# Four column tiles for experts of up to 32 rows, and three split blocks ahead instead of two

## The chip, the cores and the metric

The kernel runs on one core of one Trainium2 chip. The metric is the device time of one execution in microseconds (us), taken as the median of several runs.

## What is computed

The reference is two transformer blocks, one after the other, on 512 tokens of 1024 channels. The first block is differential attention and a gated linear recurrence, merged, with an MLP behind. The second one is two kinds of attention, then a mixture of experts, then a gate. The change touches the mixture of experts alone, which is cut to this:

```python
# 512 tokens, D_MODEL = D_FF_2 = 1024, N_EXPERTS = 32, TOP_K = 4, SWIGLU_LIMIT = 7.0
logits = (xf @ w_router + b_router).astype(jnp.float32)
top_v, top_i = lax.top_k(logits, TOP_K)
w = jax.nn.softmax(top_v, axis=-1)
...
h = lax.ragged_dot(xs, w_up, sizes) + b_up[sorted_e]
g, lin = jnp.split(h, 2, axis=-1)
g = jnp.minimum(g, SWIGLU_LIMIT)
lin = jnp.clip(lin, -SWIGLU_LIMIT, SWIGLU_LIMIT)
act = g * jax.nn.sigmoid(SWIGLU_ALPHA * g) * (lin + 1.0)
y = lax.ragged_dot(act, w_down, sizes) + b_down[sorted_e]
y = y * w.reshape(-1)[order][:, None].astype(y.dtype)
return jax.ops.segment_sum(y, tok, num_segments=n).reshape(B, T, D)
```

The 2048 rows (512 tokens, four experts each) fall on the 32 experts as the data has it. With the inputs that are timed, 12 experts have over 64 rows (127 for the first in line, then 149, 143, 130, 126, 121, 101, 101, 87, 87, 82 and 74), and 20 have 64 or fewer: 9, 12, 19, 26, 29, 29, 29, 30, 31, 33, 36, and nine from 40 to 63.

## The kernel before

An expert's weights are 12 blocks of 1 MiB, eight of the upward product and four of the downward one (`ORDER`). Each block is fetched by one transfer on SP's queue (`fetch`, L1122) into one of eight raw buffers, block n into buffer n mod 8. So block n + 8 can be fetched when block n is done with; `refill(n)` does that. The raw buffers are halves of the tiles b1, pp, b3 and b0.

The experts stand in an order that the kernel computes on the chip from the row counts (`order`). Two forms of expert exist:

- A **large expert** (`expert`, over 64 rows) works on 128 rows in three products of split numbers. `unfold` splits a raw block into a high part (ACT, L219) and a low part (DVE, L220); four pairs of buffers hold such parts: two named wh and wl, one named raw, one in b2. `part` (L1316 the bias, L1322) then does 12 matmuls of 128x512 for a block: high by high, low by high, and high by the rows' low part. In the loop over its 12 blocks, the split of block i + 2 stands ahead of the matmuls of block i. In the first four pairs a large expert may have more than 128 rows; `second` does these with 16 matmuls of 128x128 a block, on four column tiles of 32 rows (L1476, L1482), directly from the raw block, which is refilled only then.
- A **small expert** (`few`, 64 rows or fewer) reads the raw blocks directly: `halves` (L1517 the bias, L1521) does eight matmuls of 128x256 a block on two column tiles of 64 rows each.

After the upward blocks 1, 3, 5 and 7 (small: 3, 5 and 7) follows the gate (`swiglu` or `gated`): steps on ACT (L1345, L1346) and on DVE (L1347 to L1349), then transposes on PE and a copy or split (`flip`) give the rows of the downward product. The last of these, after block 7, feeds blocks 10 and 11.

`places` runs the first expert, then a chain of nested conditions `pairs(t)` (L1235). In it a small expert and a large one alternate, the smallest with the largest first, while `nP > t`; nP, a count that the chip computes, is 11 for these inputs. I call them pair 1 to pair 11 (t = 0 to 10). The remaining small experts come out of a tree of conditions, `rest` (L1243). In a paired small expert, blocks 10 and 11 are followed by the splits of the next large expert's first two blocks, and its rows are flipped (`ahead`, L1303) at blocks 8 and 9. Instructions run in program order on each engine; a scheduler sets that order from the code when the program is built, within one arm of a condition.

Of the kernel before, what the change touches and what calls it, by code (L numbers as in the profile page):

```python
# [157 lines left out]
class K:  # L158
# [944 lines left out]
    RAW, PAIRS = 8, 4  # L1103
# [38 lines left out]
    def moe(self):  # L1142
        tc, nc, a = self.tc, self.nc, self.a
        with ExitStack() as es:
# [52 lines left out]
            for n in range(2):  # L1197
                self.unfold(n)
# [10 lines left out]
    def places(self, srt):  # L1209
# [41 lines left out]
        pairs(0)  # L1251
# [106 lines left out]
    def finish(self, e, big):  # L1358

        nc, m = self.nc, self.m  # L1360
        sl, i = m["sl"][e // 4 % 2], e % 4
        if big:
            for c in range(2):
                nc.scalar.activation(m["y"][0][:, 512 * c:512 * c + 512], self.bank(e, 8 + c), AF.Copy, scale=sl["w"][:, i:i + 1])
            self.scatter(m["y"][0], sl, i)
        else:
            for c in range(2):
                p, w = self.bank(e, 8 + c), sl["w"][:64, i:i + 1]
                nc.scalar.activation(m["y"][0][:64, 512 * c:512 * c + 256], p[:64, :256], AF.Copy, scale=w)
                nc.vector.tensor_scalar(m["y"][0][:64, 512 * c + 256:512 * c + 512], p[64:, :256], w, None, op0=OP.mult)  # L1370
            self.scatter(m["y"][0], sl, i, 64)
# [44 lines left out]
    def expert(self, e, two=False):  # L1416
# [7 lines left out]
        for i in range(12):  # L1424
            n = e * 12 + i
            if i < 10:
                self.split(*self.pairs[(n + 2) % self.PAIRS], self.raw(n + 2))
                if not two:
                    self.refill(n + 2)
            if i < 2 and not two:  # L1430
                self.refill(n)
# [5 lines left out]
            if i == 0 and e:  # L1437
                self.finish(e - 1, False)
# [6 lines left out]
        self.finish(e, True)  # L1445
# [59 lines left out]
    def halves(self, p, x, i, e):  # L1505
# [5 lines left out]
        o = p[:64, :256], p[64:, :256]  # L1511

        cut = lambda w, n: self.cut(w, up, j, n, 2)
# [425 lines left out]
```

## Time and profile before

| what | us |
|---|---|
| median of three runs (2597.35 to 2602.37) | 2599.8 |
| the profiled execution | 2600.15 |
| its span, first to last instruction | 2598.1 |
| first small expert starts | 1385.37 |
| last pair ends | 2214.8 |

The mixture of experts fills the stretch from about 1340 to 2490 us. A timeline row gives the start of an operation, its duration, its engine and line, the tiles that it writes and reads, how often it stands there in a row, and in brackets the idle time of the engine before it with what ended it. A matmul in 32-bit floats counts as two in such a row: "x32" on L1482 is one block's 16 matmuls. "PE" is the matrix engine, "mm", "lg" and "pv" are its accumulators, "SPq" is SP's queue of issued transfers. The start of the next small expert is the end of a pair.

### The profile page before, as it was taken

How to read it: one execution, taken by the hardware profiler on the slowest of the kernel's cores; microseconds unless marked ns; L12 is line 12 of the kernel's file. 1: busy time of each engine (PE TensorE's matmuls, PEld its weight loads, DVE VectorE, ACT ScalarE, POOL GpSimd, SP SyncE). 2: the span in 40 equal slices, each digit the busy share in tenths (PEclk: the TensorE clock that was granted, in tenths of full speed). 3: DMA queues.
4: the chain of work that ended last, by engine and by line, in shares of the span. 5: the costliest groups of instructions: out<-in, count | busy, mean ns of one | idle time of the engine just before them, and what ended most of it. 6: DMA issues, size and time to landing. Idle time of an engine off the chain costs nothing. (4 is left out here: it accounts for less than half of the span.)

```text
span 2598.1 us, 41846 instructions
## 1 busy us (share of the span) xinstructions
PE 2425.4 (93%) x17042; PEld 1941.2 (75%) x17042; DVE 1326.2 (51%) x2473; ACT 1043.5 (40%) x1578; POOL 174.5 (7%) x184
## 2 busy tenths in 40 slices
PE   7999999999999999999989999999999999788888
PEld 5789987898898898898976676666666666554557
DVE  6767753344333344557585466445656666121135
ACT  5755552223223324557353344334444444111133
POOL 0021100000000000000010010110001000000000
PEclk9999999999999999999979999999999999899999
DMA  4122222322222222220378889989999999799990
GB/s 160 65 90 78 74 70 89 127 86 88 98 93 86 98 70 83 75 71 17 109 271 324 305 317 333 341 301 367 381 378 392 385 403 373 294 399 400 407 376 33
DMA packets 86474, 552.63 MB, mean 213 GB/s; under 512 B 11799, under 2 KB 12951, under 8 KB 24936
## 3 DMA queue, kind: packets, MB, share of 16 engines
q1 hardware_dynamic: 71280, 508.33, 50.6%
q0 software_dynamic: 8352, 29.76, 4.7%
q10 hardware_dynamic: 6616, 11.53, 1.3%
q8 instruction: 142, 2.33, 0.4%
q14 instruction: 84, 0.69, 0.1%
HBM read 530.03 MB, written 19.55 MB: 212 GB/s over the span
## 5 line engine op out<-in xcount | busy, mean ns | idle before, releaser
L245 PE MATMUL mm<-b,wh 128*128 128x512 f32 (+1 forms) x1840 | 512.8, 365 | 1.7 <-ACT b L222 0.8
L245 PEld LDWEIGHTS mm<-b,wh 128*128 128x128 f32 x1840 | 328.8, 190 | 65.4 <-issue 3.4
L245 PE MATMUL mm<-b,wl 128*128 128x512 f32 (+2 forms) x920 | 335.2, 365 | 1.3 <-DVE wl L205 1.3
L245 PE MATMUL mm<-wh,b 128*128 128x256 f32 x1488 | 284.3, 287 | 1.5 <-DVE b L675 0.8
L205 DVE TENSOR_TENSOR wl<-raw,wh 128x2048 fp32r<-128x2048 f32 x81 | 185.5, 2290 | 176.2 <-ACT wh L204 176.2
L204 ACT ACTIVATE wh<-raw 128x2048 fp32r<-128x2048 f32 x81 | 155.1, 1915 | 261.2 <-PE mm L245 248.8
L245 PEld LDWEIGHTS mm<-wh,b 128*128 128x128 f32 x1488 | 235.9, 191 | 4.6 <-DVE b L675 1.2
L245 PE MATMUL mm<-wl,b 128*128 128x256 f32 x744 | 213.0, 286 | 1.0 <-DVE wl L205 1.0
L220 DVE TENSOR_TENSOR wl<-b,wh 128x2048 fp32r<-128x2048 f32 x74 | 169.2, 2288 | 65.4 <-ACT wh L219 62.4
L245 PEld LDWEIGHTS mm<-b,wl 128*128 128x128 f32 (+1 forms) x920 | 174.6, 190 | 31.8 <-DVE wl L205 2.2
L1521 PE MATMUL lg<-b,xf 128*64 128x256 f32 x1280 | 154.3, 389 | 14.7 <-DMA b<-w_up 10.1
L219 ACT ACTIVATE wh<-b 128x2048 fp32r<-128x2048 f32 x74 | 141.0, 1908 | 61.8 <-DMA b<-w_up 30.8
L245 PEld LDWEIGHTS mm<-wl,b 128*128 128x128 f32 x744 | 141.9, 191 | 2.5 <-DVE wl L205 1.3
L1521 PEld LDWEIGHTS lg<-b,xf 128*64 128x64 f32 x1280 | 94.3, 139 | 65.7 <-DMA b<-w_up 15.9
L1521 PE MATMUL lg<-b,b 128*64 128x256 f32 x1024 | 130.7, 394 | 7.5 <-DMA b<-w_dn 7.2
L213 POOL TENSOR_TENSOR rs<-rm,c_nhalf 128x1 f32<-128x1 f32 (+3 forms) x52 | 53.0, 1021 | 1158.9 <-DVE rm L211 1150.6
L1521 PEld LDWEIGHTS lg<-b,b 128*64 128x64 f32 x1024 | 76.0, 141 | 49.1 <-issue 11.5
L1345 ACT ACTIVATE sg<-mm,seven 128x128 f32<-128x128 f32 (+2 forms) x48 | 21.8, 455 | 223.2 <-PE mm L1521 180.9
L1521 PE MATMUL mm<-pp,xf 128*64 128x256 f32 x640 | 84.3, 388 | 4.6 <-DMA pp<-w_up 4.5
L1347 DVE SCALAR_TENSOR_TENSOR sg<-lg,sg 128x256 f32<-128x256 f32 (+1 forms) x48 | 19.2, 399 | 127.6 <-ACT sg L1346 127.6
L1521 PE MATMUL mm<-b,xf 128*64 128x256 f32 x640 | 74.8, 383 | 7.0 <-DMA b<-w_up 7.0
L1345 ACT ACTIVATE sg<-lg,seven 128x256 f32<-128x256 f32 (+1 forms) x48 | 21.7, 452 | 146.1 <-PE lg L1521 118.4
(534 smaller groups left out, 4597.9 us busy)
## 6 DMA issues: line engine op xcount, KB each, us to landing
b<-w_up SPq DMA_DIRECT2D x190, 1024.0 KB, 6.7
b<-w_dn SPq DMA_DIRECT2D x96, 1024.0 KB
pp<-w_up SPq DMA_DIRECT2D x64, 1024.0 KB, 13.4
raw<-w_in SPq DMA_DIRECT2D x39, 1024.0 KB, 4.9
pp<-w_dn SPq DMA_DIRECT2D x32, 1024.0 KB, 14.2
raw<-w_up SPq DMA_DIRECT2D x16, 1024.0 KB, 5.8
raw<-w_down SPq DMA_DIRECT2D x16, 1024.0 KB, 4.8
raw<-w_out SPq DMA_DIRECT2D x8, 1024.0 KB, 4.8
```

The source lines that it names most:

```text
L204: nc.scalar.activation(wh, raw, AF.Copy)
L205: nc.vector.tensor_tensor(wl, raw, wh.bitcast(F32), op=OP.subtract)
L213: self.nc.gpsimd.tensor_tensor(r, m, self.c["nhalf"][:, :n], op=OP.pow)
L219: nc.scalar.activation(hi, src, AF.Copy)
L220: nc.vector.tensor_tensor(lo, src, hi.bitcast(F32), op=OP.subtract)
L245: self.nc.tensor.matmul(ps, l, r, start=(i == 0), stop=(i == n - 1))
L1345: nc.scalar.activation(sg, pg, AF.Relu, scale=-1.0, bias=m["seven"][:rows, 0:1])
L1347: nc.vector.scalar_tensor_tensor(sg, pg, 7.0, sg, op0=OP.min, op1=OP.mult)
L1521: nc.tensor.matmul(o[n], x(4 * kh + k), cut(w[:, k], n), start=not up and kh == k == 0, stop=kh == 1 and k == 3)
```

## The change

- **Four column tiles.** `few`, `pieces` (was `halves`) and `finish` take a number of tiles, `of`. With `of` = 4 a small expert of up to 32 rows does 16 matmuls of 128x128 a block, on four tiles of 32 rows each; its result is scaled in four pieces of 32x128 for each half.
- **A chain of its own.** `order` computes a further count, nT: how many of the pairs, from the first on, have a small expert of up to 32 rows. It is 9 here. `tiny` is the nested chain for these, with four tiles; nP is loaded behind it, and the other pairs come out of a new tree of conditions, `pairs(lo, hi)`, with two tiles. `rest` stays as it was.
- **Three blocks ahead.** `LEAD` is 3: the first three blocks of a large expert are split in the preceding small one (before the first expert, in the stretch that computes the order), and in the expert the split of block i + 3 stands ahead of block i. In pairs without rows over 128 each split is followed by the refill of its raw buffer.
- **The flip earlier.** The rows of the next large expert are flipped at blocks 4 and 5 of the preceding small one, not 8 and 9.

```diff
@@ moe, unfold @@
-    RAW, PAIRS = 8, 4
+    RAW, PAIRS, LEAD = 8, 4, 3
...
-    def unfold(self, n):
+    def unfold(self, n, keep=False):
         wh, wl = self.pairs[n % self.PAIRS]
         self.split(wh, wl, self.raw(n))
-        if n % 12 > 1 or n >= NE * 12:
+        if not keep:
             self.refill(n)
...
-            for n in range(2):
-                self.unfold(n)
+            for n in range(self.LEAD):
+                self.unfold(n, keep=True)
@@ places @@
-        nP = load(1, 15)
-
-        def pairs(t):
+        nT = load(3, 15)
+
+        def pair(t, of):
+            self.few(1 + 2 * t, True, t < self.SECOND, of)
+            self.expert(2 + 2 * t, t < self.SECOND, of)
+
+        def tiny(t):
             if t < NE // 2 - 1:
-                with tc.If(nP > t):
-                    self.few(1 + 2 * t, True, t < self.SECOND)
-                    self.expert(2 + 2 * t, t < self.SECOND)
-                    pairs(t + 1)
+                with tc.If(nT > t):
+                    pair(t, 4)
+                    tiny(t + 1)
+
+        def pairs(lo, hi):
+            if hi - lo > 1:
+                mid = (lo + hi) // 2
+                with tc.If(nT < mid):
+                    pairs(lo, mid)
+                with tc.If(nP > mid):
+                    pairs(mid, hi)
+            else:
+                with tc.If(nT < lo + 1):
+                    with tc.If(nP > lo):
+                        pair(lo, 2)
...
-        pairs(0)
+        tiny(0)
+        nP = load(1, 15)
+        pairs(0, NE // 2 - 1)
         rest(0, NE // 2 - 1)
@@ finish @@
+        rows, y = 128 // of, m["y"][0]
+        w = sl["w"][:rows, i:i + 1]
+        for c in range(2):
+            for g in range(of):
+                p, o = self.bank(e, 8 + c)[rows * g:rows * g + rows, :512 // of], y[:rows, 512 * c + 512 // of * g:][:, :512 // of]
+                if g % 2:
+                    nc.vector.tensor_scalar(o, p, w, None, op0=OP.mult)
+                else:
+                    nc.scalar.activation(o, p, AF.Copy, scale=w)
+        self.scatter(y, sl, i, rows)
@@ expert @@
-            if i < 10:
-                self.split(*self.pairs[(n + 2) % self.PAIRS], self.raw(n + 2))
-                if not two:
-                    self.refill(n + 2)
-            if i < 2 and not two:
+            if i + self.LEAD < 12:
+                self.unfold(n + self.LEAD, keep=two)
+            if i < self.LEAD and not e:
                 self.refill(n)
@@ halves, now pieces @@
-        for k in range(4):
-            for n in range(2):
-                nc.tensor.matmul(o[n], x(4 * kh + k), cut(w[:, k], n), start=not up and kh == k == 0, stop=kh == 1 and k == 3)
+        for k in range(4):
+            for g in range(of):
+                nc.tensor.matmul(o[g], x(4 * kh + k), self.cut(w[:, k], up, j, g, of), start=not up and kh == k == 0,
+                                 stop=kh == 1 and k == 3)
@@ few @@
-            self.halves(self.bank(e, i), (lambda k: xf[:, k]) if i < 8 else h, i, e)
+            self.pieces(self.bank(e, i), (lambda k: xf[:, k, :rows]) if i < 8 else h, i, e, of)
             self.refill(n)
-            if i > 9 and (paired or e == NE - 1):
+            if paired and i + self.LEAD > 11:
+                self.unfold(n + self.LEAD, keep=second)
+            if e == NE - 1 and i > 9:
                 self.unfold(n + 2)
...
-            self.ahead(e, i, 8, paired)
+            self.ahead(e, i, 4 if paired else 8, paired)
@@ order @@
+        v.tensor_scalar(gt[:, 2], key[:, 1:], 32 * 32 + 31.5, None, op0=OP.is_lt)
...
+        v.tensor_tensor(of[:, 3:4], nP, tiny, op=OP.min)
```

The scheduler puts the instructions of a pair into another order. On PE, at the seam from the second pair's small expert to its large one (b_12343 or b_12345 and b_12206 are raw buffers in b0 and b1, wh and wl a split block, L1521 the small expert's blocks and L1482 the rows over 128), before:

```order
7446 L1521 MATMUL lg<-b_12343,b_12234 64x256 x16
7447 L1459 MATMUL tr<-c_ident,b_12234 128x32 x8
7448 L1316 MATMUL mm<-bup,one_12237 128x512
7449 L1322 MATMUL mm<-wh,b_12232 128x512
7450 L1322 MATMUL mm<-wl,b_12232 128x512
7451 L1322 MATMUL mm<-wh,b_12232 128x512 x2
7452 L1322 MATMUL mm<-wl,b_12232 128x512
...
7458 L1476 MATMUL pv<-bup,one_12237 32x128 x4
7459 L1482 MATMUL pv<-b_12206,xs 32x128 x32
7460 L1322 MATMUL mm<-wh,b_12232 128x512
```

And after, where L1535 is the line of the small expert's blocks, L1497 that of the rows over 128, and L1339 that of the large expert:

```order
7452 L1535 MATMUL lg<-b_12345,b_12234 32x128 x16
7453 L1474 MATMUL tr<-c_ident,b_12234 128x32 x8
7454 L1333 MATMUL mm<-bup,one_12237 128x512
7455 L1491 MATMUL pv<-bup,one_12237 32x128
7456 L1535 MATMUL lg<-b_12345,b_12234 32x128 x16
7457 L1491 MATMUL pv<-bup,one_12237 32x128 x7
7458 L1333 MATMUL mm<-bup,one_12237 128x512
7459 L1333 MATMUL lg<-bup,one_12237 128x512 x2
7460 L1497 MATMUL pv<-b_12206,xs 32x128 x16
7461 L1339 MATMUL mm<-wh,b_12232 128x512
7462 L1497 MATMUL pv<-b_12206,xs 32x128 x13
7463 L1339 MATMUL mm<-wl,b_12232 128x512
```

The rows over 128 of block 0, and all but a few of block 1, now stand ahead of the first split block's matmuls. They stood behind it.

On ACT, in the seventh pair's large expert, from the split of its block 5 on, before (b_12225 and b_12343 hold raw blocks 4 to 7, b_12206 blocks 8 and 9, pp blocks 10 and 11; b_12224 is the fourth split pair; "sg" are steps of the gate, and "h<-tr" is the flip behind it):

```order
1183 L219 ACTIVATE raw<-b_12343 128x2048
1184 L219 ACTIVATE b_12224<-b_12343 128x2048
1185 L1345 ACTIVATE sg<-lg,seven 128x256
1186 L219 ACTIVATE h<-tr 128x512
1187 L1346 ACTIVATE sg<-sg,seven 128x256
1188 L219 ACTIVATE raw<-pp 128x2048
1189 L219 ACTIVATE wh<-b_12206 128x2048
1190 L1345 ACTIVATE sg<-lg,seven 128x256
1191 L1346 ACTIVATE sg<-sg,seven 128x256
1192 L219 ACTIVATE b_12224<-pp 128x2048
1193 L219 ACTIVATE wh<-b_12206 128x2048
1194 L219 ACTIVATE h<-tr 128x256 x2
```

And after, from the splits of blocks 4 and 5 on:

```order
1193 L219 ACTIVATE wh<-b_12225 128x2048 x2
1194 L219 ACTIVATE wh<-b_12206 128x2048
1195 L219 ACTIVATE h<-tr 128x512
1196 L219 ACTIVATE raw<-b_12345 128x2048
1197 L1362 ACTIVATE sg<-lg,seven 128x256
1198 L1363 ACTIVATE sg<-sg,seven 128x256
1199 L219 ACTIVATE wh<-b_12206 128x2048
1200 L219 ACTIVATE b_12224<-b_12345 128x2048
1201 L219 ACTIVATE raw<-pp 128x2048
1202 L1362 ACTIVATE sg<-lg,seven 128x256
1203 L219 ACTIVATE b_12224<-pp 128x2048
1204 L1363 ACTIVATE sg<-sg,seven 128x256
```

Block 8 (wh from b_12206) was split behind blocks 6 and 7 (raw and b_12224 from b_12343); now it stands ahead of both. Block 11 (b_12224 from pp) stood behind both steps of the last gate; now it stands between the two. On DVE the low parts follow in the same order, and the last gate's three steps come behind block 11's. On PE block 8 now runs among block 6's matmuls and block 9 among block 7's, where both stood behind block 7.

## Rows read from the trace of the kernel before

**Rows 1.** page, part 1: busy us (share of the span) xinstructions

```profile
PE 2425.4 (93%) x17042; PEld 1941.2 (75%) x17042; DVE 1326.2 (51%) x2473; ACT 1043.5 (40%) x1578; POOL 174.5 (7%) x184
```

**Rows 2.** stretches: us, busy us of each engine, clock, DMA share, GB/s

```profile
1400.00:1500.00 100.00, 95.09 (x939) 65.36 (x936) 55.77 (x99) 44.28 (x52) 8.20 (x7) 0.99 0.91 341
...
1900.00:2000.00 100.00, 92.20 (x509) 66.56 (x508) 64.67 (x76) 51.38 (x50) 6.80 (x4) 0.98 0.98 390
```

**Rows 3.** PE, start of seven small experts: start us, us, line, xcount

```profile
1385.37 0.65 PE L1517 MATMUL lg<-bup,one 128*64 128x256 f32 x4
...
1467.41 0.65 PE L1517 MATMUL lg<-bup,one 128*64 128x256 f32 x4
...
1550.93 0.65 PE L1517 MATMUL lg<-bup,one 128*64 128x256 f32 x4
...
1721.18 0.65 PE L1517 MATMUL lg<-bup,one 128*64 128x256 f32 x4
...
1864.06 0.65 PE L1517 MATMUL lg<-bup,one 128*64 128x256 f32 x4
...
1934.82 0.65 PE L1517 MATMUL lg<-bup,one 128*64 128x256 f32 x4
...
2073.86 0.65 PE L1517 MATMUL lg<-bup,one 128*64 128x256 f32 x4
```

**Rows 4.** PE's timeline, second pair; in brackets idle time, releaser

```profile
1467.89 3.62 PE L1521 MATMUL lg<-b,xf 128*64 128x256 f32 x32
...
1496.73 0.68 PE L1459 MATMUL tr<-c_ident,b 32*128 32x32 f32 x8 [4.08 <-DVE b L220]
...
1498.26 0.63 PE L1322 MATMUL mm<-wl,b 128*128 128x512 f32 x1
...
1504.21 0.50 PE L1322 MATMUL mm<-wh,b 128*128 128x512 f32 x1
...
1507.45 1.06 PE L1482 MATMUL pv<-pp,xs 128*32 128x128 f32 x32
...
1508.77 2.97 PE L1322 MATMUL mm<-raw,b 128*128 128x512 f32 x12
```

**Rows 5.** timeline of PE, seventh pair

```profile
1911.04 0.60 PE L1303 MATMUL tr<-c_ident,b 128*128 128x128 f32 x4
...
1917.94 0.46 PE L1303 MATMUL tr<-c_ident,b 64*128 64x64 f32 x4
...
1921.20 0.79 PE L1322 MATMUL mm<-wl,h 128*128 128x512 f32 x1 [2.23 <-DVE wl L220]
...
1925.41 0.60 PE L1303 MATMUL tr<-c_ident,b 128*128 128x128 f32 x4
```

**Rows 6.** timeline of ACT, seventh pair

```profile
1886.93 1.91 ACT L219 ACTIVATE wh<-b 128x2048 fp32r<-128x2048 f32 x1 [1.88 <-DMA b<-w_up]
```

**Rows 7.** timeline of DVE, seventh pair

```profile
1888.88 2.29 DVE L220 TENSOR_TENSOR wl<-b,wh 128x2048 fp32r<-128x2048 f32 x1 [3.10 <-ACT wh L219]
...
1921.40 0.41 DVE L1347 SCALAR_TENSOR_TENSOR sg<-lg,sg 128x256 f32<-128x256 f32 x1
```

**Rows 8.** timeline of SP's queue, seventh pair: fetches of 1 MiB

```profile
1866.47 5.95 SPq L1122 DMA_DIRECT2D b<-w_dn  x4
1874.24 2.06 SPq L1122 DMA_DIRECT2D b<-w_up  x2
```

**Rows 9.** transfers in 40 slices of 1862 to 1936 us

```profile
GB/s 430 341 71 133 301 308 359 303 421 412 407 416 421 416 425 416 430 416 425 412 416 379 312 421 430 430 430 430 416 421 421 416 421 412 425 173 407 425 425 407
```

**Rows 10.** PE, from the last pair to the remaining small experts

```profile
2211.84 2.96 PE L1322 MATMUL mm<-b,h 128*128 128x512 f32 x12
2226.92 1.12 PE L1517 MATMUL lg<-bup,one 128*64 128x256 f32 x4 [12.12 <-DVE one L1286]
2229.47 6.25 PE L1521 MATMUL lg<-b,xf 128*64 128x256 f32 x32 [1.43 <-SPq L1243]
```

**Rows 11.** branches of that place on PE's queue: xcount, ns min/median/max

```profile
L1243 PEldq COMPARE_BRANCH  x4: 70/2311/4560, 2216.9 to 2226.6; - x4
```

More of the change, by code (lines that the diff above doesn't have):

```diff
@@ L1356, in bank, with finish @@
         return mm[(s + i % 2) % 4]
-    def finish(self, e, big):
+    def finish(self, e, of=2):
         nc, m = self.nc, self.m
         sl, i = m["sl"][e // 4 % 2], e % 4
[L1362 to L1371, printed above, removed]
+        rows, y = 128 // of, m["y"][0]
[8 more added lines that the diff above has]
+        self.scatter(y, sl, i, rows)
     def numbers(self, e):
@@ L1414, in last, with expert @@
             self.split(self.y[0][:64, cc], self.y[1][:64, cc], y)
-    def expert(self, e, two=False):
+    def expert(self, e, two=False, of=2):
         nc, m = self.nc, self.m
@@ L1503, in second_finish, with pieces @@
         self.scatter(m["actb"][0], m["sl"][2], 0, 32)
-    def halves(self, p, x, i, e):
+    def pieces(self, p, x, i, e, of):
         nc = self.nc
@@ L1510, in halves @@
         kh, j = (c % 2, c // 2) if up else ((i - 8) // 2, 0)
-        o = p[:64, :256], p[64:, :256]
-        cut = lambda w, n: self.cut(w, up, j, n, 2)
+        r = 128 // of
+        o = [p[r * g:r * g + r, :512 // of] for g in range(of)]
         if up and kh == 0:
             b = self.bup.bitcast(F32)[:, 512 * (j // 2):512 * (j // 2) + 512]
-            for n in range(2):
-                nc.tensor.matmul(o[n], self.m["one"][e % 2].bitcast(F32)[:, j % 2, :64], cut(b, n), start=True, stop=False)
+            for g in range(of):
+                nc.tensor.matmul(o[g], self.m["one"][e % 2].bitcast(F32)[:, j % 2, :r], self.cut(b, up, j, g, of), start=True, stop=False)
@@ L1518, in halves @@
         w = self.raw(e * 12 + i).rearrange("p (k f) -> p k f", k=4)
         for k in range(4):
-            for n in range(2):
-                nc.tensor.matmul(o[n], x(4 * kh + k), cut(w[:, k], n), start=not up and kh == k == 0, stop=kh == 1 and k == 3)
-    def few(self, e, paired=False, second=False):
+            for g in range(of):
+                nc.tensor.matmul(o[g], x(4 * kh + k), self.cut(w[:, k], up, j, g, of), start=not up and kh == k == 0,
+                                 stop=kh == 1 and k == 3)
@@ L1525, in few @@
+    def few(self, e, paired=False, second=False, of=2):
         nc, m = self.nc, self.m
         self.numbers(e)
-        xf, act = m["xf"], m["act"][0][:, :512]
-        hf = m["y"][0][:, :512].rearrange("p (t a r) -> p t a r", t=4, a=2)
-        h = lambda k: hf[:, k % 2, k // 2] if k < 4 else hf[:, k % 2 + 2, k // 2 - 2]
+        rows, q = 128 // of, 4 // of
+        xf, act = m["xf"], m["act"][0][:, :1024 // of]
+        hf = m["y"][0][:, :2 * q * 128].rearrange("p (t a r) -> p t a r", t=2 * q, a=of)
+        h = lambda k: hf[:, k % q + q * (k // 4), k % 4 // q]
@@ L1542, in few @@
                 j = i // 2
[L1543 to L1544 removed]
+                w = 256 // of
+                pg, pl = [self.bank(e, k)[:, :2 * w] for k in (0, 2)] if j == 1 else [self.bank(e, i)[:, w * k:w * k + w] for k in range(2)]
                 self.gated(pg, pl, self.side(act, j, 64))
             if i in (5, 8, 9):
[L1547 removed]
+                t0, t1 = {5: (0, q), 8: (q, q + 1), 9: (q + 1, 2 * q)}[i]
                 p = self.tr()
@@ L1748, in order @@
         key, t32, P, P2 = [S2[:, o:o + n] for o, n in ((0, 32), (32, 32), (64, 32), (96, 64))]
-        gt = S2[:, 160:222].rearrange("p (a e) -> p a e", a=2)
+        gt = S2[:, 160:253].rearrange("p (a e) -> p a e", a=3)
         col = [S2[:, 284 + i:285 + i] for i in range(12)]
         kc, big, q1, g, sb, far, ex = col[:7]
-        r4 = S2[:, 296:298]
-        r, na = [r4[:, i:i + 1] for i in range(2)]
+        r4 = S2[:, 296:299]
+        r, na, tiny = [r4[:, i:i + 1] for i in range(3)]
         of = self.ovf
```

18 lines of the change are left out of this document (8 added, 10 removed).

## The prediction, made before the changed kernel ran

> **What bounds the kernel now.** The page says PE is busy 93% of the span [rows 1], which suggests that fewer PE steps mean less time. The table by stretch corrects that: in the first pairs the transfers are busy 0.91 of the time at 341 GB/s, in the later ones 0.98 at 390 GB/s [rows 2]. The timelines then show how the two take turns. I use three stretches [rows 3]:
>
> - pairs 1 to 4: 1385.37 to 1721.18, 335.8 us, 84.0 each;
> - pairs 5 to 9: 1721.18 to 2073.86, 352.7 us, 70.5 each;
> - pairs 10 and 11: from 2073.86 to the end of the last block at 2211.84 + 2.96 = 2214.8 [rows 10], 140.9 us, 70.5 each.
>
> At the seam inside a pair PE waits for a transfer. In the second pair it has no work for 4.08 us, until the low part of the large expert's block 0 is made [rows 4]. In the seventh, ACT has sat idle until that block landed and starts its high part at 1886.93, 22.9 us after the pair began [rows 3, 6]; the low part ends 4.2 us later [rows 7]. From 1866.47 on SP issues the fetches ahead of it, the small expert's blocks 8 to 11 and then this one (at 1874.24) [rows 8]. Each is issued when a small block is done with its buffer, and five of 1.05 MB at the 420 GB/s of a full slice take 12.5 us; the slices at 71 and 133 GB/s fall where the previous result is scattered and rows are gathered [rows 9]. So the small expert's matmuls do not set the seam. The start of its *first* block does, through the fetch that this block frees, and then the transfers. Behind the seam the large expert runs on PE, fed by splits in the order in which ACT and DVE make them.
>
> **Four column tiles.** A small block of 16 recorded matmuls costs 3.62 / 2 = 1.81 us on two tiles; the nearest row for four tiles is the block of the rows over 128, 1.06 us [rows 4]. That is 0.75 a block and 9.0 an expert. I do not count 9.0: only the first block's share moves the first fetch, with its bias 0.8 to 1.1 us. I take 1.1, and put the high part of block 0 at 21.8 to 22.8 us into a pair, mean 22.3; the low part is then ready at 26.5. The bounds of this edit in a pair are 0 and 9.0 us. I stay near the low one, since ACT and PE already wait for the transfer there.
>
> **Pairs 1 to 4, the seam.** In the second pair the first matmul on a low part came 30.85 us after the start (1498.26 - 1467.41) [rows 3, 4]. Block 0 and the rows over 128 of blocks 0 and 1 then took 5.95 until 1504.21, of which 2 x 1.06 were those rows; the block alone took 3.8 instead of 2.97, as its first matmuls ran slower after the wait. From 1504.21 to the pair's end at 1550.93 there are 46.7 us. In the new order the rows over 128 of blocks 0 and 1 fill the wait. The period becomes 26.5 + 3.9 + 46.7 = 77.1, some 77.5 with what is left of block 1's. Four pairs: 4 x (84.0 - 77.5) = **-26** (-34 to -14: the seam two us earlier, or only the 2.1 us moved and one gained by the fetch). The third split costs ACT 1.9 us and DVE 2.3, which wait there anyway [rows 6, 7].
>
> **Pairs 5 to 9, the order of the splits.** Here the large expert has no rows over 128, and the scheduler has put block 8's split ahead of block 6's, and block 11's between the steps of the last gate. I follow the seventh pair from the start of block 0's high part (0). Before: block 5 done at 24.1 (1911.04), block 7 at 31.0 (1917.94), last flip at 38.5 (1925.41), end at 47.9 (1934.82) [rows 3, 5, 6]. After, with 1.91 a high part, 2.29 a low part, 2.97 a block of matmuls and 0.41 a gate step of DVE [rows 4, 6, 7]:
>
> - First low part 4.2, blocks 0 to 3 until 17.0, block 4 until about 20.3, block 5 until 23.7: as before.
> - Block 8's high part needs the pair that block 4 frees: 20.3 to 22.2. Behind it on ACT stand the flip's high part (to 22.9) and block 6's (to 24.8). On DVE block 8's low part ends at 24.6, the flip's at 25.3, block 6's at 27.6. Block 6 ends on PE at 30.
> - On DVE four short steps and block 9's low part (to 31.6) stand ahead of block 7's (to 33.9): block 7 ends at 36.5, 5.5 later than before, with blocks 8 and 9 done in between.
> - Then ACT does the gate's first step (37.1) and the whole high part of block 11 (39.0), DVE its low part (41.3), and only then the gate's steps on DVE (42.6), transposes and flip (44.2). PE has nothing left but blocks 10 and 11, which need this: it is idle for about 6.8 us. Before, blocks 8 and 9 stood there and hid it.
> - Blocks 10 and 11: 5.9, and 1.5 to 2 more at the lower speed that rows 5 show after a wait of 2.23. End at 52.0, against 47.9.
>
> With block 0 at 22.3 the period is 74.3, against 70.5: 5 x 3.8 = **+19** (+5 to +33: blocks 8 and 9 run later than they could and hide half of the stall; or each of the three waits slows PE by 2 us more). The earlier refills make no transfer late that was in time: 26 MB at 390 GB/s are under 68 us.
>
> **Pairs 10 and 11** stand on two tiles, block 0 at 22.9, with the same new order: 2 x 4.4 = **+9** (+2 to +14).
>
> **The new tree.** From the last pair to the remaining small experts PE is idle for 12.12 us, waits 1.43 more, and its first two blocks take 6.25 instead of 3.62 [rows 4, 10]: 12.1 + 2.1 (until 2229.47, less the usual 0.5 of bias) + 2.6 = 16.8. It follows three conditions that are false across a long way: the chain's end and two of the tree, of which one takes 4.56 us and one that is not taken 0.07 [rows 11]. The seam from pair 9 to pair 10 now has the same kind: the end of `tiny`, then the arms for pairs 1 to 7 and 8 to 9 skipped. The later seam keeps its three. So **+16.5** (+13 to +20), once; a further load of a count lies in it. The Trainium skill ("Runtime: NRT & Kernel Launch", Instruction fetch mechanics) speaks against this edit: a taken branch whose target is not in the two pages at hand waits for a transfer of the target's page. By that rule alone the seam costs three such transfers, with the trace's 4.56 us 13.7, and the sum would be 3 lower; the trace agrees with the rule, and shows what the slow restart adds to it.
>
> **The rest.** The scaling of a small result in four pieces, and the flip at blocks 4 and 5, lie where ACT and DVE are idle (ACT 40% and DVE 51% busy [rows 1]); nothing. If that cover is gone, the flip costs under 2 us a pair. Three steps for the new count and one split more ahead of the first expert: 0 to 2.3 [rows 7], **+1**.
>
> **Sum:** -26 + 19 + 9 + 16.5 + 1 = +19.5, on the profiled 2600.15: **2619**. The profiled run lies 0.35 above the median of the runs shown, which makes no difference here.
>
> **The rivals.**
> - *Faster: the order of the splits costs nothing, since PE takes blocks 8 and 9 into the waits.* Then the later pairs are bound by transfers, at 69 us: 7 x -1.5 = -10, and -26 - 10 + 16.5 + 1 = -19: 2581 (2565 to 2594). For it: DMA is the fuller resource there, 0.98 [rows 2]. Against: the stall of the last gate has no block left to hide it. It decides where that stall is under 2 us a pair. 0.16.
> - *The whole saving of four tiles shows.* The Trainium skill ("TensorEngine Tiling (Array Packing)", Theoretical Speedup) gives up to 4x for 32 rows where 64 give 2x. As a mechanism of this kernel: if PE and not the transfer set the seam, nine pairs would each be 9.0 shorter, -81 + 9 + 16.5 + 1: 2546. Against: the waits of rows 4 and 6, and the rows' 1.81 to 1.06 is less than that factor. 0.03.
> - *No change:* half the stalls are hidden, -26 + 9 + 4 + 16.5 + 1 = +5, or the seam gains 5 more: 2595 to 2605. 0.13.
> - *Slower by twice as much:* PE falls to its lower speed at each of the three waits in the seven later pairs, 2 us more each, 7 x 4 = 28: 2647. For it: rows 5 and 10 show slow matmuls after waits of 2.23 and 12.12. Against: the first waits are short. 0.15.
> - *The change does not do what it says:* the four tiles run one after the other, the small expert is no shorter, and of the gain only the 2 x 1.06 of the rows over 128 remains, 4 x -2.1: 2637. Against: the 1.06 of rows 4. 0.03.
>
> **How the numbers follow.** The forecast's own band, 2605 to 2637, gets 0.50. The range goes from 2584 to 2650: it leaves out the whole-saving rival, most of the faster one's lower half and the far end of the slow one. About 0.2% of the time (5 us) is what a measurement can tell from no change. Faster, below 2594.6: 0.16 + 0.03 = 0.19. Same: 0.13. Slower: 0.50 + 0.15 + 0.03 = 0.68.
>
> **What would show it.** In the new profile, block 0's high part should start 21.8 to 22.8 us into each of the first nine pairs; small blocks should take 1.06 us; pairs 1 to 4 last 77.5, 5 to 9 last 74.3, 10 and 11 last 74.9. A new idle stretch of PE of about 7 us should end with the flip behind the last gate, with block 11's split ahead of it on ACT and DVE, and one of 12 us stand between pairs 9 and 10. The forecast is wrong if that stall is absent, if block 0 lands much earlier than 21 us into a pair, or if the later pairs last under 70.

## The result, and the profile after

The changed kernel is slower: its median is 2627.75 us (2622.08 to 2632.06) against 2598.57 (2593.83 to 2602.37), a ratio of 1.0114 with a 95% interval of 1.0091 to 1.0136. The forecast was 2619, slower than before. The span of its profiled execution is 2629.6 us, 31.5 more than before, and PE is busy for less of it, as the page's first part shows (against [rows 1]):

```profile
PE 2368.0 (90%) x18896; PEld 1924.0 (73%) x18896; DVE 1316.2 (50%) x2484; ACT 1042.0 (40%) x1596; POOL 171.9 (7%) x184
```

PE is busy for 57 us less (2425.4 before), and the span is longer all the same. The lengths of the pairs tell where. These are the first bias rows of five small experts on PE's timeline, as in [rows 3]:

```profile
1383.66 0.42 PE L1531 MATMUL lg<-bup,one 128*32 128x128 f32 x8 [0.29 <-DVE oh L1858]
...
1461.64 0.43 PE L1531 MATMUL lg<-bup,one 128*32 128x128 f32 x8
...
1703.32 0.42 PE L1531 MATMUL lg<-bup,one 128*32 128x128 f32 x8
...
1857.87 0.43 PE L1531 MATMUL lg<-bup,one 128*32 128x128 f32 x8
...
1933.60 0.43 PE L1531 MATMUL lg<-bup,one 128*32 128x128 f32 x8
```

Pairs 1 to 4 took 1703.32 - 1383.66 = 319.7 us, 16.2 less than before. Pair 9 ended at 2083.8 (below), so pairs 5 to 9 took 380.5, which is 27.8 more.

**The seam inside a pair.** On PE's timeline the second pair now reads as follows; [rows 4] are its rows of before.

```profile
1461.88 1.93 PE L1535 MATMUL lg<-b,xf 128*32 128x128 f32 x64
...
1478.86 2.77 PE L1535 MATMUL lg<-b,b 128*32 128x128 f32 x42 [5.19 <-DVE b L1570]
...
1488.02 1.08 PE L1497 MATMUL pv<-b,xs 128*32 128x128 f32 x32
...
1491.33 0.50 PE L1339 MATMUL mm<-wl,b 128*128 128x512 f32 x1 [0.81 <-DVE wl L220]
```

Two small blocks take 1.93 us (x64), half of the 3.62 (x32 each) that two tiles took, and the small expert is nevertheless not done sooner: PE waits 5.19 us for DVE. The rows over 128 (L1497) now stand ahead of the first low part, as the built order said. On DVE the reason for the wait stands in brackets:

```profile
1478.52 0.29 DVE L1570 COPY b<-tr 128x128 f32<-128x128 f32 x1 [9.11 <-DMA acc<-b,s0i]
```

L1570 copies the small expert's flipped gate rows into the tile y. The previous large expert's result lies there too, and its scatter ("acc<-b") still reads it until 1478.5, 16.9 us into the pair. Two tiles came to this copy later and met the scatter in three of the nine pairs; four tiles wait for it in all nine. The list of waits from the first to the ninth pair (engine, tile and line, then what ended the wait: us in all, times, longest) gives the sum. Before:

```profile
DVE b L1551 <- DMA acc<-b,s1i: 8.4, 2, 4.3
...
DVE b L1551 <- DMA acc<-b,s0i: 7.2, 1, 7.2
```

After:

```profile
DVE b L1570 <- DMA acc<-b,s0i: 28.2, 5, 9.1
PE tr L1320 <- DVE b L1366: 27.9, 5, 5.6
...
DVE b L1570 <- DMA acc<-b,s1i: 24.6, 4, 8.9
```

That is 15.6 us in three pairs before and 52.8 us in all nine now. Block 0's high part starts 25.7 us into these pairs in the mean, where it was 23.5.

The transfer of block 0 is fetched earlier and lands no earlier. In the seventh pair SP issues it at 1864.09, 6.2 us into the pair, where it was 10.2 [rows 3, 8]:

```profile
1864.09 1.96 SPq L1122 DMA_DIRECT2D b<-w_up  x2
```

By the last completion event of its transfer it lands 24.4 us into the second pair, as before (24.4), and 23.7 us in the mean of the first six pairs and the eighth (23.6 before; of the seventh and the ninth some events are missing). Before, ACT waited for the transfer in eight of the nine pairs, as in [rows 6]. Now it does so in four; in the second, third, fifth, seventh and ninth pair the high part follows at once behind the last of the four pieces of the small expert's scaling (L1387), as the ACT rows below show for the seventh, and block 0 has landed before. This is longest in the third and the fifth pair, where the high part starts at 28.7 and 29.0, 5.8 and 7.2 us behind the landing.

**The last gate.** The row of PE (L1320) in the list of waits after the change is the other wait: five of 5.58 us each, one in each of the pairs 5 to 9. In the seventh pair, on PE, ACT and DVE in turn (against [rows 5 to 7]):

```profile
1913.93 0.62 PE L1339 MATMUL mm<-wh,h 128*128 128x512 f32 x2
...
1919.65 0.40 PE L1339 MATMUL mm<-wh,h 128*128 128x512 f32 x1
1925.63 1.11 PE L1320 MATMUL tr<-c_ident,b 128*128 128x128 f32 x4 [5.58 <-DVE b L1366]
1926.79 4.08 PE L1339 MATMUL mm<-raw,h 128*128 128x512 f32 x12
1930.71 2.96 PE L1339 MATMUL mm<-b,h 128*128 128x512 f32 x12
```

```profile
1883.58 0.36 ACT L1387 ACTIVATE b<-lg,s1w 32x128 f32<-32x128 f32 x1 [0.47 <-DVE b L1385]
1883.84 3.69 ACT L219 ACTIVATE wh<-b 128x2048 fp32r<-128x2048 f32 x2
...
1919.85 0.47 ACT L1362 ACTIVATE sg<-lg,seven 128x256 f32<-128x256 f32 x1 [3.80 <-PE lg L1339]
1920.22 1.90 ACT L219 ACTIVATE b<-pp 128x2048 fp32r<-128x2048 f32 x1
1922.02 0.50 ACT L1363 ACTIVATE sg<-sg,seven 128x256 f32<-128x256 f32 x1
```

```profile
1871.21 0.29 DVE L1570 COPY b<-tr 128x128 f32<-128x128 f32 x1 [5.21 <-DMA acc<-b,s1i]
...
1922.15 2.29 DVE L220 TENSOR_TENSOR b<-pp,b 128x2048 fp32r<-128x2048 f32 x1 [3.36 <-ACT b L219]
1924.36 0.42 DVE L1364 SCALAR_TENSOR_TENSOR sg<-lg,sg 128x256 f32<-128x256 f32 x1
```

Block 11's high part (b<-pp, 1920.22) runs between the gate's two steps on ACT (1919.85 and 1922.02), and its low part (1922.15) ahead of the gate's on DVE (1924.36). PE, which has only blocks 10 and 11 left, gets its transposes at 1925.63, and the block behind them takes 4.08 us, the next one 2.96 again.

**The new tree.** Between pairs 9 and 10, on PE, and its branches on PE's queue (xcount, ns least/median/longest), against [rows 10, 11]:

```profile
2080.84 2.96 PE L1339 MATMUL mm<-b,h 128*128 128x512 f32 x12
2098.15 1.12 PE L1531 MATMUL lg<-bup,one 128*64 128x256 f32 x4 [14.35 <-ACTq L1246]
2099.06 5.64 PE L1535 MATMUL lg<-b,xf 128*64 128x256 f32 x32
2104.53 0.60 PE L1531 MATMUL lg<-bup,one 128*64 128x256 f32 x4
...
2108.42 0.60 PE L1531 MATMUL mm<-bup,one 128*64 128x256 f32 x4
```

```profile
L1246 PEldq COMPARE_BRANCH  x4: 68/2072/5056, 2084.7 to 2094.7; - x4
```

PE is idle for 14.35 us, and from 2098.15 to the second block's bias it needs 6.38 us, 2.5 more than the next block (3.89). One false condition that skips a long arm took 5.06 us here, and the shortest branch 0.07.

### The profile page after: what moved, and what is told of

It reads as the page before. It is cut to its first block, busy times and chain, and to the rows that moved or that the text cites. A ratio compares the mean times of both kernels' runs of the same rounds, so it can differ in the third digit from the quotient of the medians.

```text
span 2629.6 us, 45778 instructions
## 1 busy us (share of the span) xinstructions
PE 2368.0 (90%) x18896; PEld 1924.0 (73%) x18896; DVE 1316.2 (50%) x2484; ACT 1042.0 (40%) x1596; POOL 171.9 (7%) x184
## 3 DMA queue, kind: packets, MB, share of 16 engines
q1 hardware_dynamic: 71280, 508.33, 49.8%
## 5 line engine op out<-in xcount | busy, mean ns | idle before, releaser
L219 ACT ACTIVATE wh<-b 128x2048 fp32r<-128x2048 f32 x74 | 139.7, 1905 | 53.8 <-PE lg L1339 26.7
L1535 PE MATMUL lg<-b,xf 128*32 128x128 f32 (+1 forms) x1856 | 127.5, 322 | 15.0 <-DMA b<-w_up 10.9
L1535 PE MATMUL lg<-b,b 128*32 128x128 f32 (+1 forms) x1600 | 108.7, 336 | 25.7 <-DVE b L1570 12.1
L1535 PEld LDWEIGHTS lg<-b,xf 128*32 128x32 f32 (+1 forms) x1856 | 86.3, 123 | 47.5 <-DMA b<-w_up 16.5
L1535 PEld LDWEIGHTS lg<-b,b 128*32 128x32 f32 (+1 forms) x1600 | 71.6, 129 | 47.8 <-DVE b L1570 13.6
L1362 ACT ACTIVATE sg<-mm,seven 128x64 f32<-128x64 f32 (+3 forms) x48 | 20.9, 436 | 199.3 <-PE mm L1535 131.2
L1339 PE MATMUL mm<-wh,b 128*128 128x512 f32 x192 | 74.9, 461 | 6.1 <-ACT wh L219 6.1
L1535 PE MATMUL mm<-pp,xf 128*32 128x128 f32 (+1 forms) x928 | 72.6, 335 | 8.0 <-DMA pp<-w_up 5.1
L220 DVE TENSOR_TENSOR b<-pp,b 128x2048 fp32r<-128x2048 f32 x26 | 59.5, 2290 | 33.0 <-ACT b L219 33.0
```

The lines of the kernel that those rows point to most:

```text
L219: nc.scalar.activation(hi, src, AF.Copy)
L220: nc.vector.tensor_tensor(lo, src, hi.bitcast(F32), op=OP.subtract)
L1339: nc.tensor.matmul(p, s[:, kk], w[:, k], start=not up and kk == j == 0, stop=kk == KC - 1 and j == len(terms) - 1)
L1362: nc.scalar.activation(sg, pg, AF.Relu, scale=-1.0, bias=m["seven"][:rows, 0:1])
L1535: nc.tensor.matmul(o[g], x(4 * kh + k), self.cut(w[:, k], up, j, g, of), start=not up and kh == k == 0, stop=kh == 1 and k == 3)
```

## The experiments

All changes are against the changed kernel unless said otherwise. This table holds what the timelines of the profiled runs give: means of the length of a pair (from one small expert's first bias row to the next), of the start of block 0's high part in it (the first L219 of a raw block), and of the rest from there on. Pair 9 is left out, since the new seam lies at its end. The runs were made in several sessions, in which the kernel before had medians of 2597.1 to 2602.8 us; so a difference of under 5 us between two medians of different sessions shows little. The ratios in brackets are to the kernel before in the same session.

| kernel | median us | pairs 1-4: length, block 0, rest | pairs 5-8: length, block 0, rest |
|---|---|---|---|
| before | 2598.6 | 84.0, 23.9, 60.1 | 70.5, 23.4, 47.1 |
| changed | 2627.75 | 79.9, 25.8, 54.1 | 76.2, 25.6, 50.6 |
| e1 one chain | 2615.0 | 79.4, 25.7, 53.7 | 75.8, 25.1, 50.7 |
| e2 flipped rows apart | 2618.25 | 78.8, 25.1, 53.7 | 74.2, 23.9, 50.4 |
| e3 gate first | 2614.75 | 79.6, 25.9, 53.7 | 73.9, 25.4, 48.5 |
| e4 splits in order | 2605.6 | 80.0, 26.3, 53.7 | 71.8, 24.8, 47.0 |
| e5 two tiles | 2638.05 | 82.6, 24.6, 58.0 | 75.3, 23.8, 51.5 |
| e6 two blocks ahead | 2583.9 | 80.0, 26.2, 53.8 | 68.6, 25.2, 43.3 |
| e7 flip late | 2638.4 | 82.0, 28.3, 53.7 | 77.4, 26.9, 50.5 |
| e8 = e1 + e2 + e4 | 2586.5 | 78.8, 25.1, 53.7 | 71.7, 24.0, 47.7 |
| e9 = e6 + e2 | 2577.1 | 78.7, 25.0, 53.7 | 68.0, 24.5, 43.5 |
| e10 = e6 + e2 + e1 | 2562.5 | 78.5, 24.8, 53.7 | 67.5, 24.2, 43.3 |
| e11 = e6 + e5 | 2592.0 | 83.8, 25.2, 58.6 | 67.5, 23.9, 43.7 |
| e12 early flip alone | 2598.4 | 83.0, 24.8, 58.1 | 70.9, 23.8, 47.1 |

### What the tree costs

```diff
-                with tc.If(nT > t):
-                    pair(t, 4)
+                with tc.If(nP > t):
+                    pair(t, 4 if t < 9 else 2)
...
-        tiny(0)
-        nP = load(1, 15)
-        pairs(0, NE // 2 - 1)
+        tiny(0)
```

> The changed kernel with one nested chain for all eleven pairs: the number of tiles (four for the first nine, two for the others) is written into the program, which fits these inputs alone, and the new tree of conditions is gone. If the tree costs what its seam shows (PE idle for 14.35 us between pairs 9 and 10 and a slow first pair of blocks, 5.64 instead of 3.62), the time falls by 15 to 17 us, to 2611 to 2613. If the transfers that rest meanwhile must catch up or the far branch is paid elsewhere, it falls by under 8 us.

It came to 2615.03 (ratio to before 1.0059, 1.0042 to 1.0076): 12.7 less by the medians, 18.5 by the spans (2611.1 and 2629.6). The expected 15 to 17 lie between the two. Runs of one kernel lie some 5 us to either side of its median, so both agree with the 16.9 of the seam. That the transfers catch up meanwhile, the second case (under 8), is out.

### What the scatter costs

```diff
-        hf = m["y"][0][:, :2 * q * 128].rearrange("p (t a r) -> p t a r", t=2 * q, a=of)
+        hf = m["act"][0][:, 512:512 + 2 * q * 128].rearrange("p (t a r) -> p t a r", t=2 * q, a=of)
```

> The changed kernel with the small expert's flipped gate rows put into the unused half of the tile act, not into y, from which the previous large expert's result is still being scattered. Theory: DVE's copy of these rows waits for that scatter (5.21 us in the seventh pair, 9.11 in the second), all that is queued behind it on DVE and PE is late, and block 0's high part starts 25.4 to 26 us into a pair although the block landed at 21.3 to 22.1. Then the high part starts at about 23.5, 2 to 3 us earlier in nine pairs: 18 to 27 us less, 2601 to 2610. Rival, the prediction's: the transfers alone set the seam, and the time stays within 5 us of 2628.

It came to 2618.25 (1.0073, 1.0048 to 1.0098), 9.5 less: half of what the theory wanted, and beyond the rival's 5. DVE no longer waits for the scatter in these pairs. What waits instead is shown on PE's timeline of the same second pair:

```profile
1479.40 1.27 PE L1535 MATMUL lg<-b,b 128*32 128x128 f32 x32 [1.31 <-DMA b<-w_dn]
1482.90 1.06 PE L1474 MATMUL tr<-c_ident,b 32*128 32x32 f32 x8 [2.24 <-DMA b<-xs,s2i]
```

Now one of the small expert's own last blocks ("b<-w_dn") and the rows over 128 ("b<-xs,s2i") are what PE waits for. So in pairs 1 to 4 block 0's high part gained 0.7 us (25.8 to 25.1), and in pairs 5 to 8 it gained 1.7. Nearly all of this lies in two pairs, the third (28.7 to 25.3) and the fifth (29.0 to 22.8). In the others the scatter ended little later than what came behind it: with the rows apart, block 0 lands at 24.0 us in the mean of the same seven pairs (the first six and the eighth), and its high part starts 0.5 us behind that. The theory wanted 23.5 because it took block 0 to have landed at 21.3 to 22.1; the last completion events stand at 24.4 for the second pair, and at 23.2 or later for the seventh.

### What the order of the splits costs

```diff
                 if i + self.LEAD < 12:
-                    self.unfold(n + self.LEAD, keep=two)
+                    with ExitStack() as es:
+                        for ins in () if two or e == 0 or i != 8 else self.gate:
+                            es.enter_context(self.tc.issue_after(ins.ins))
+                        self.unfold(n + self.LEAD, keep=two)
```

`self.gate` holds the last gate's last instructions on ACT and DVE.

> The changed kernel with block 11's split held behind the last gate's steps on ACT and on DVE, in the large experts without rows over 128. Theory: PE's idle 5.58 us ahead of the last transposes, and the slow blocks behind it (4.08 instead of 2.97), come from block 11's split between the gate's steps; without it the gate ends 3.6 to 4.2 us earlier in seven pairs, but block 11's low part is then needed at once, some 2 us after block 10's matmuls begin. Gain 2.5 to 4 us a pair, 17 to 28 us: 2600 to 2611. Rival: the stall is that of block 7's late split, and the split that was held back only waits elsewhere: under 7 us in all.

It came to 2614.75 (1.0059, 1.0041 to 1.0077), 13.0 less, or 1.9 in each of seven pairs: less than the theory's 17, more than the rival's 7. The wait for the gate is shorter by 3.5 us, but part of it came back in slow matmuls and two short waits, the last for block 11's low part, on PE's timeline of the seventh pair:

```profile
1915.46 0.66 PE L1319 MATMUL tr<-c_ident,b 128*128 128x128 f32 x4 [2.12 <-DVE b L1365]
1916.37 1.22 PE L1338 MATMUL mm<-raw,h 128*128 128x512 f32 x2 [0.26 <-ACT h L219]
...
1918.34 0.80 PE L1338 MATMUL mm<-b,h 128*128 128x512 f32 x1 [0.32 <-DVE b L219]
```

The second of this kind also holds block 8's split behind block 7's:

```diff
+                        behind = () if two or e == 0 else self.gate if i == 8 else split if i == 5 else ()
```

> As the one before, with block 8's split held behind block 7's too, so that the splits come in the order of before. Theory: block 7 then ends 3 to 5 us earlier, and blocks 8 and 9 stand behind it and hide the gate: the large expert takes 48 us from block 0's high part, as before the change, against 49.8 now. Together 2 to 4.5 us a pair, 14 to 30 us: 2598 to 2614. Rival: the order of blocks 6 to 9 costs nothing, and this gives what the run with the gate alone gives, within 5 us.

2605.64 (1.0033, 1.0015 to 1.0051): 22.1 less, as the theory had it. The rest of a pair behind block 0's high part is 47.0 us, what it was before the change. So the order of the splits, not the four tiles, took the later pairs from 47.1 to 50.6, and the order of blocks 6 to 9 has 9 us of it. One stall is left that the order of before did not have, on DVE, in the seventh pair:

```profile
1899.84 0.42 DVE L1323 COPY xf<-tr 128x256 f32<-128x256 f32 x1 [2.01 <-PE tr L1319]
1900.18 2.28 DVE L219 TENSOR_TENSOR raw<-b,raw 128x2048 fp32r<-128x2048 f32 x1
```

The copy of the next rows (L1323) stands ahead of block 6's low part and waits 2.01 us for its transposes. PE then waits for that low part:

```profile
1902.52 3.79 PE L1338 MATMUL lg<-raw,b 128*128 128x512 f32 x11 [2.28 <-DVE raw L219]
```

### Which part of the change moved the splits

```diff
-    RAW, PAIRS, LEAD = 8, 4, 3
+    RAW, PAIRS, LEAD = 8, 4, 2
```

> The changed kernel with two blocks split ahead, not three; four tiles, both chains and the early flip stay. In the built order of this one block 6's split stands ahead of block 8's again and block 11's behind the last gate. Theory: the third block ahead is what moved the splits, and the large experts without rows over 128 take 47 to 48.5 us from block 0's high part on, not 50.5: 2.5 to 3.5 us less in seven pairs, 2603 to 2612. In pairs 1 to 4 the third block brings nothing, since the rows over 128 cover it. Rival: the third block ahead is needed to keep PE busy behind the seam, and the time is no less than 2622.

2583.89, a ratio to before of 0.9946 (0.9927 to 0.9966): 43.9 less than the changed kernel, and faster than before the change. Both expectations missed it, by 19 us on the near side. The third block ahead is by far the dearest part of the change. Half of its 44 us is the order of the splits, by the run before this one; of the other half the traces show the wait of 2.28 us, which is gone here, and the rest of it stays unexplained. That the rest would be 47 to 48.5 us was wrong as well; it is 43.3, below that of before. On PE's timeline the seventh pair has next to no waits left behind the seam:

```profile
1901.95 0.73 PE L1339 MATMUL mm<-raw,h 128*128 128x512 f32 x2 [0.26 <-ACT h L219]
...
1903.46 0.50 PE L1339 MATMUL mm<-b,h 128*128 128x512 f32 x1 [0.55 <-DVE b L220]
```

### Four tiles and the early flip

```diff
-                    pair(t, 4)
+                    pair(t, 2)
```

> The changed kernel with two column tiles of 64 rows in the nine pairs as well; the chain, the tree, the three blocks ahead and the early flip stay. Theory: the transfers and not PE set the seam inside a pair, so the 9 us of PE time that four tiles save in a small expert were hidden anyway, and the copy that waits for the scatter comes later by itself: the time stays within 8 us of 2627.75. Rival: four tiles are what made pairs 1 to 4 shorter (4.0 us each), and nine pairs lose 4 to 9 us: 2660 or more.

2638.05 (1.0152, 1.0116 to 1.0188), 10.3 more, a little beyond the theory's 8 and far from the rival's 2660. So four tiles bring something, about a sixth of the PE time that they save (PE is busy for 2431.4 us here, for 2368.0 with four). It lies in pairs 1 to 4 (79.9 against 82.6 us, 10.7 in all), in the rest behind block 0 (54.1 against 58.0). There it is again an order that moved: on PE's timeline of the second pair the rows over 128 of blocks 0 and 1 stand behind the first split block, at 35.2 us, where four tiles have them in the wait for its low part (1488.02 above).

```profile
1500.36 1.93 PE L1497 MATMUL pv<-b,xs 128*32 128x128 f32 x64
```

In pairs 5 to 8, which have no such rows, two tiles are no slower (75.3 against 76.2). Then the flip at its old place:

```diff
-            self.ahead(e, i, 4 if paired else 8, paired)
+            self.ahead(e, i, 8, paired)
```

> The changed kernel with the large expert's rows flipped at blocks 8 and 9 of the small one, as before the change. Theory: at blocks 4 and 5 the flip lies in idle time of ACT and DVE, and at 8 and 9 it lies beside the wait for the transfers as well: within 5 us of 2627.75. Rival: the early flip makes the gain of pairs 1 to 4, since the transposed rows over 128 are ready sooner: 8 us or more slower.

2638.36 (1.0145, 1.011 to 1.018), 10.6 more: the rival. But not by its reason. The rest of pairs 1 to 4 is the same 53.7; block 0's high part starts 2.5 us later (28.3). On DVE, in the second pair, both halves of the flip now come behind the copy that waits for the scatter, one after the other, and the split behind them:

```profile
1478.86 0.29 DVE L1570 COPY b<-tr 128x128 f32<-128x128 f32 x1 [12.39 <-DMA acc<-b,s0i]
...
1482.85 0.69 DVE L220 TENSOR_TENSOR b<-tr,b 128x512 fp32r<-128x512 f32 x1
1485.04 0.69 DVE L220 TENSOR_TENSOR b<-tr,b 128x512 fp32r<-128x512 f32 x1 [1.50 <-ACT b L219]
...
1490.90 4.49 DVE L220 TENSOR_TENSOR wl<-b,wh 128x2048 fp32r<-128x2048 f32 x2 [1.45 <-issue]
```

Two tiles with two blocks ahead:

> Two blocks ahead and two column tiles everywhere; the tree and the early flip stay. With three blocks ahead, four tiles were worth 10.3 us (2638.05 - 2627.75). Theory: with the splits in order, the four tiles also let the small expert's last blocks end before the first split is there, and PE is what bounds the large expert behind the seam; so they are worth more, 20 to 35 us: 2604 to 2619, slower than before the change by the tree. Rival: the transfers hide them as they did, and it gives 2590 to 2598.

2591.99 (0.9957, 0.9941 to 0.9973), 8.1 more than with four tiles, and in the rival's range. The two are of different sessions; by their ratios to the kernel before they are 3 us apart, and the intervals overlap. So four tiles are worth no more here than with three blocks ahead, and by how much less is not shown. This run has pairs 5 to 8 at 67.5 us, so these too owe their speed to something other than the tiles. One candidate was the early flip, alone on the kernel before:

```diff
-            self.ahead(e, i, 8, paired)
+            self.ahead(e, i, 4 if paired else 8, paired)
```

> The kernel before, with one part of the change alone: the large expert's rows are flipped at blocks 4 and 5 of the paired small one, not 8 and 9. Two tiles, the one old chain, two blocks split ahead and their refills as before. Two blocks ahead with two tiles, the tree and the early flip gave 2592.0 with later pairs of 66 to 68.6 us, and the tree costs 13 to 17 us. Theory: the early flip is what shortens the later pairs (70.5 before), by taking its low parts on DVE out from between the first splits: 2574 to 2582. Rival: the earlier refills of the first two raw buffers, which this one leaves out, did that: 2592 to 2600.

2598.37, beside 2602.79 for the kernel before on the same chip: 0.9985 (0.997 to 0.9999), 4 us, and within the rival's range. The rest of pairs 5 to 8 stays at 47.1. What this run and the one with two tiles and two blocks ahead do not share is the place of the first refills, and the tree, which lies behind pair 9. In pairs 5 to 8 the refills are thus the one difference, and these last 70.9 us here and 67.5 there. The kernel before refilled the raw buffers of blocks 0 and 1 at their matmuls. Its fetches in the seventh pair, on SP's queue, then those of the run with two tiles and two blocks ahead:

```profile
1894.15 1.63 SPq L1122 DMA_DIRECT2D b<-w_up  x2
1896.40 0.33 SPq L1122 DMA_DIRECT2D pp<-w_dn  x1
1896.94 0.33 SPq L1122 DMA_DIRECT2D b<-w_dn  x1
```

```profile
1889.94 0.33 SPq L1122 DMA_DIRECT2D b<-w_dn  x1
...
1891.23 0.33 SPq L1122 DMA_DIRECT2D b<-w_dn  x1
1893.99 2.93 SPq L1122 DMA_DIRECT2D pp<-w_dn  x2
```

Before, block 10 (pp<-w_dn) was fetched ahead of block 8 (b<-w_dn), is split ahead of it in the built order, and block 9's low part came too late: PE waited 2.23 us for it in [rows 5], and again with the early flip alone:

```profile
1914.41 0.79 PE L1322 MATMUL mm<-wl,h 128*128 128x512 f32 x1 [2.22 <-DVE wl L220]
```

With the refill right behind the split, blocks 8 and 9 are fetched and split ahead of 10, and the wait is gone. By difference this is worth the 6.4 us between these two runs plus the 13 to 17 of the tree, some 20 us. The place of the refills was not run alone.

### Together

> Three remedies together: one nested chain (number of tiles written into the program for these inputs), the small expert's flipped rows in the tile act, and the splits in the order of before. Alone they brought 12.7, 9.5 and 22.1 us off 2627.75. If they act in places of their own, this gives 2627.75 - 44 = 2583, below the kernel before. If the flipped rows and the order share a wait, or the transfers become the bound of the later pairs at about 69 us, it gives 2590 to 2600.

2586.46 (0.9957, 0.9932 to 0.9981): 41 of the 44 us add up, within the noise all of them, so the three act in places of their own. The same place is reached more simply with two blocks ahead:

> Two blocks ahead and the small expert's flipped rows in the tile act, with four tiles, the tree and the early flip of the changed kernel. Two blocks ahead alone gave 2583.9, where DVE still waits 4.75 us for the scatter in the eighth pair. If that wait is worth here what it was worth alone (9.5 us), 2574. If the later pairs, now at 67.4 to 70.4 us, are bound by the transfers, only pairs 3 and 5 gain (high part of block 0 at 28.4 and 27.4 us, against 24 to 25): 2577 to 2582.

2577.12 (0.9889, 0.9855 to 0.9922), at the fast end of its second case. Pairs 3 and 5 gained most (82.0 to 79.2 and 70.4 to 67.4) and pair 4 1.8, the others little, much as the second case says.

> As the one before with one nested chain (number of tiles written into the program for these inputs), no tree. If the tree's seam costs here what it cost alone (12.7 us by the medians, 16.9 by the profile), this is 12 to 17 us below the one before: 2558 to 2568, and the fastest of all. If the transfers use the seam to catch up, under 8 us.

2562.54 (0.9849, 0.9823 to 0.9876): 14.6 less again, the fastest of all, 1.5% below the kernel before; its one chain fits these inputs alone. In its later pairs the transfers leave no room, as the table by stretch says (columns as in [rows 2]; the last two are DMA share and GB/s):

```profile
1800.00:1900.00 100.00, 90.10 (x742) 67.89 (x742) 69.46 (x91) 53.73 (x53) 4.91 (x4) 0.94 1.01 402
```

## Why the prediction was right, and which steps were not

The forecast was +19.5 us on the profiled execution; its span grew by 31.5. Direction and range held. The terms were these; both terms of the pairs came out some 9 to 10 us too dear, each still inside the range that it was given, and smaller misses the other way took a third off that:

| term | forecast | profile after |
|---|---|---|
| pairs 1 to 4 | -26 | -16.2 |
| pairs 5 to 9 | +19 | +27.8 |
| seam between pairs 9 and 10 | +16.5 | +16.9 |
| pairs 10 and 11, without the slow start | +9 | +6.0 |
| ahead of the first pair | +1 | -1.7 |
| behind the last pair | 0 | -1.2 |

- **The new tree** was right, in place, cause and size: 14.35 + 2.5 = 16.9, and the run without it was 12.7 us faster by the medians and 18.5 by the spans. Three false conditions were reckoned at the rows of the old seam. The Trainium skill ("Runtime: NRT & Kernel Launch", Instruction fetch mechanics) says that a taken branch to a target outside the two pages at hand waits for a transfer of that page. The trace agrees in that the branches differ so much: 5.06 us for the longest and 0.07 for the shortest.
- **The order of the splits** was right as a mechanism. In the seventh pair the steps were forecast at 23.7, 30, 36.5 and 52.0 us behind block 0's high part for blocks 5, 6 and 7 and the end; they came at 23.4, 30.1, 35.8 and 49.8. The stall of 6.8 was 5.58. The end was 2.2 early: block 7 came 0.7 sooner, the stall was 1.2 shorter, and the slow stretch behind it, put at 1.5 to 2, was 1.1. Undoing the order gave 22 us back.
- **The step that failed is the seam inside a pair.** "I take 1.1, and put the high part of block 0 at 21.8 to 22.8 us into a pair": it came at 25.7, 2.2 later than before and not 1.2 earlier. The miss of 3.4 us in nine pairs is 31 us, against the 11 to 12 that the shorter rest gave back there (54.1 against 55.2 in pairs 1 to 4, and 50.6 against 52.0 in 5 to 8). It has two parts. First, 1.4 us is the landing of block 0: the fetches did move (the small expert's first one from 2.4 to 1.7 us into the seventh pair, block 0's own from 10.2 to 6.2), but block 0 lands at 23.7, where it landed before. "Only the first block's share moves the first fetch" is true, and that the landing follows the fetch is what fell; what holds the transfers up between the two was not isolated. Second, 2.0 us is the time for which block 0 lies landed while ACT is not ready for it. The prediction went on "since ACT and PE already wait for the transfer there" and put the small result's scaling at nothing. It did not ask what the small expert, made faster, would meet: the tile y, still being read by the scatter. PE, DVE and then the scaling on ACT, ahead of the high part, are late by that in five pairs. With the flipped rows apart the second part falls to 0.5 us, and the kernel gains 9.5 us; the first part stays.
- **That four tiles' 9.0 us an expert would not show** was right: the run with two tiles is 10 us slower, where 81 would have been the whole. That the prediction's 1.1 us a pair from the first fetch makes the same 10 us in nine pairs is luck: with two tiles block 0's high part starts earlier (24.5 and 23.8 us), and the 10 us lie in where the rows over 128 stand. The Trainium skill ("TensorEngine Tiling (Array Packing)", Theoretical Speedup) has up to 4x for a dimension of up to 32 and up to 2x for up to 64, a factor of two between them. The rows give 3.62 / 1.93 = 1.9 for the block and nothing like it for the pair.
- **What the prediction did not price** is that the refill right behind the split changes the order of the fetches. "The earlier refills make no transfer late that was in time" passes over that they make blocks 8 and 9 early; with two blocks ahead this is the largest gain of the change, some 20 us by the difference of two runs. With three ahead the later pairs do not show it. Added up from single runs, the change holds parts worth some 35 us (four tiles, early flip, refills), and two that cost 60 (the third block ahead and the tree).

Of the rivals, the faster one fell by the 5.58 us that no block hides. The one with slow matmuls after each wait (2647) priced what did not happen: after the gate's wait the slow stretch was 1.1 us. That the four tiles run one after the other fell by the 1.93 us of two small blocks, and that their whole saving shows by the 10 us of the run with two tiles.

Left open: whether the place of the refills alone, on the kernel before, gives the 20 us that the difference of two runs says; why block 0 lands no earlier though it is fetched earlier; and where the half of the third block's 44 us goes that the order of the splits does not explain, beyond the copy of the next rows ahead of block 6's low part.

## What to carry to other kernels

When a stage is made shorter, look not only at what it waits for but at what its first writes land on: a buffer shared with an outgoing transfer may have cost nothing only because the stage was slow. How many blocks are split ahead and where their buffers are refilled both moved the built order of later splits here; read that order on each engine up to the last dependent step, and see what is left to hide it. A row of untaken branches is cheap, a skipped arm is not (0.07 us against 4 to 5 here), so choose the form of a condition by what the likely case skips.

## What was not expected of the hardware

A scatter of 128 rows holds its source for long: issued at 1466.49 for the second pair and at 1858.95 for the seventh, it let go of y at 1478.52 and 1871.21, 12.0 and 12.3 us later, while the weights' transfers ran beside it. And the slow matmuls behind a wait were fewer than reckoned: behind 5.58 us of waiting the first block took 4.08 us and the next 2.96, so 1.1 us, where the rows of before had suggested 1.5 to 2 behind a wait of 2.23.
